# Modulation of the adaptive norm: from row products on GpSimd and ScalarE to matrix products on TensorE, weights through the weight ring

## The chip, the cores and the metric

The kernel runs on one core of one Trainium2 chip. The metric is the device time of one execution in microseconds (us), from the first to the last instruction of the core, as the median of several executions. Engines are called by the profile's names: PE is TensorE (matrix products), PEld its loads of the stationary operand, DVE is VectorE, ACT is ScalarE, POOL is GpSimd, and SP is SyncE, whose queue issues the transfers (DMAs).

## The reference, cut to what matters

A sequence of 256 tokens with 1024 features goes through two layers of a first block (feed-forward, hybrid mixer, feed-forward), and then through two layers of a second block, beside a context sequence of 256 tokens. Layer 0 of the second block is an RWKV mixer, layer 1 a differential attention. Each layer of the second block has an adaptive norm: six vectors of 1024 numbers (shift, scale and gate, for the latents and for the context) come from two small products that depend on the inputs `c` and `c_ctx` alone.

```
for l in range(2):                                   # first block
    x = x + 0.5 * swiglu_ffn(rmsnorm(x, norm_ffn1[l]), ...)
    x = x + hybrid_mixer(rmsnorm(x, norm_mix[l]), ...)
    x = x + 0.5 * swiglu_ffn(rmsnorm(x, norm_ffn2[l]), ...)
x = rmsnorm(x, final_norm)
for i in range(2):                                   # second block
    mod  = silu(c) @ ada_w[i] + ada_b[i]             # [1024] @ [1024, 3072]
    shift, scale, gate = split(mod, 3)
    modc = silu(c_ctx) @ ada_w[i] + ada_b[i]
    shift_c, scale_c, gate_c = split(modc, 3)
    h  = rms_norm(x, norm_g[i]) * (1 + scale) + shift
    hc = rms_norm(xc, norm_g[i]) * (1 + scale_c) + shift_c
    y, yc = rwkv7_mixer(h, hc, ...) if i == 0 else diff_mixer(h, hc, ...)
    x = x + gate * y
    if i == 0: xc = xc + gate_c * yc
```

The change is about `mod` and `modc`: two matrices `ada_w[i]` of 1024 x 3072, 12.6 MB each, multiplied by two vectors.

## The kernel before, in words

Features lie on the 128 partitions, tokens along the free dimension; 1024 features are 8 tiles (`KD = 8`). All large products are made in float32r with both operands split into a high and a low part, three products for one: `mm3` issues high x high, high x low and low x high into the same sums.

**Weights.** The class `Weights` streams weight chunks in the order in which they are used (`plan_first`, `plan_second`). A chunk is a tile of 128 x 1024 numbers, 512 KB, in the first block (tiles `wraw`) and of 128 x 512, 256 KB, in the second (`vraw`). It lands in one of `nraw` raw tiles; ACT makes its high part (`emit_hi`: `whi<-wraw`), DVE its low part (`emit_lo`: `wlo<-wraw,whi`; in the mixers some pieces go to POOL), each piece 128 x 512. The raw tile is free once the low part is made. `RING, RING2 = (4, 5), (4, 4)`: four raw tiles and five pairs of parts in the first block, four and four in the second. A chunk added with `split=False` is used as it lies and holds its raw tile until the next chunk is asked for (`get`). All transfers are issued by SP, in one queue, in order: what waits for a free tile holds up what stands behind it.

**Order.** Nothing is scheduled by a compiler: the instructions stand on each engine as the Python code emits them. The code keeps a rough account of time (`Clock`) and uses it to decide what to emit next. Work off the main path is written as generators ("chains", each `yield` ends a step); `tick`, `until` and `arrive` emit the steps that the account holds to be ready, and pieces of the weight splitting.

**First block.** `ffn` makes 44 products of 8 x 3 matrix products [128 x 256] each (up), a SwiGLU for each pair, then 8 products of 22 x 3 (down): 1584 matrix products. `mixer` makes 20 column tiles of `w_in` (conv, pool, gate), then ten rounds of a gelu tile with the gate matrices of the recurrence (`wax`) before every fourth, a pool product (`pw`), ten gate tiles, and the products upwards and out: 1560 matrix products.

**Second block.** `rwkv` goes through eight pairs of heads (`j`): projections of both sequences (512 columns), a low-rank product (`lora`), the gate's projection, and chains (`prepare`, `products`, `inverse`, `recur`, `readout`) with small products; the results of the first pairs are stored by SP (`zs`). Then come the output product and the attention.

**The modulation before.** `ada` (line 1094) is one chain. It brings `c_ctx` and `c` to all partitions (1 MB), and `ada_w` as rows: 96 pieces of 128 output columns x 512 inputs, 256 KB each, through two tiles of its own (`adaw`). For each piece

```
G.tensor_tensor(out=prod, in0=raw, in1=cb[:, :, 512 * h:512 * h + 512], op=ALU.mult)
yield
load()
for q in range(2):
    A.activation(prod[:, q], prod[:, q], AF.Copy, accum_out=sums[:, i, q, h:h + 1])
```

so POOL multiplies 128 x 1024 numbers, and ACT sums them in two passes (the tiles `cb` and `prod` are both called `ada` in the profile). The chain takes a step only while `self.calm` is set, which `ffn` sets and clears at its last down product: it runs beside the feed-forward stages, and stands still in the mixers. The last piece of a layer is followed by four or five small DVE instructions that make `mods` and `gs`. They are needed from `enter_ctx` on (layer 0), and after the RWKV stage (layer 1).

All operations go through one helper, so the profile gives line 89 for each of them; the tile names tell them apart.

## Time and profile before

| what | value |
|---|---|
| median of 3 timed executions | 2275.19 us (2267.83 to 2288.46) |
| span of the profiled execution, first to last instruction | 2274.9 us |
| its own time beside that | none is listed; the span stands 0.3 us under the median |
| mean granted clock of PE | 0.930 of 2.4 GHz |
| busy: PE, PEld | 2106.3 us (93%), 1882.8 us (83%) |
| busy: DVE, ACT, POOL | 1717.8 us (76%), 1287.4 us (57%), 861.8 us (38%) |
| moved by DMA | 300.41 MB, mean 132 GB/s |
| `ada` on POOL | 96 instructions, 238.7 us busy |
| `ada` on ACT | 192 passes, 118.7 us busy, and 192 reads of the sums, 35.8 us |

Busy times are unions of the instructions of an engine. PE's matrix products overlap, so that one of 0.28 us follows the one before by less than half of that: PE's idle time and the count of products in a stretch say more than its busy share. The granted clock of a stretch is a mean of two levels, 1 (2.4 GHz) and 0.5 (1.2 GHz). Idle time of an engine is put down to what ended it.

### The profile page before, as it was taken

How to read it: one execution, taken by the hardware profiler on the slowest of the kernel's cores; microseconds unless marked ns; L12 is line 12 of the kernel's file. 1: busy time of each engine (PE TensorE's matmuls, PEld its weight loads, DVE VectorE, ACT ScalarE, POOL GpSimd, SP SyncE). 2: the span in 40 equal slices, each digit the busy share in tenths (PEclk: the TensorE clock that was granted, in tenths of full speed). 3: DMA queues.
4: the chain of work that ended last, by engine and by line, in shares of the span. 5: the costliest groups of instructions: out<-in, count | busy, mean ns of one | idle time of the engine just before them, and what ended most of it. 6: DMA issues, size and time to landing. Idle time of an engine off the chain costs nothing. (4 is left out here: it accounts for less than half of the span.)

```text
span 2274.9 us, 47231 instructions
## 1 busy us (share of the span) xinstructions
PE 2106.3 (93%) x18172; PEld 1882.8 (83%) x18172; DVE 1717.8 (76%) x3076; ACT 1287.4 (57%) x2970; POOL 861.8 (38%) x1063
## 2 busy tenths in 40 slices
PE   8998998998889889989999988999999998999998
PEld 7988988998889889989999967677677667777878
DVE  6689898888878888897666675765766764558896
ACT  6666684666666666765556543354454342347565
POOL 1154565344544453562001153443543542312331
PEclk9999999999999999999999996899889877869999
DMA  7666554666666565456566310101100110215542
GB/s 243 207 190 202 159 167 131 213 204 200 195 211 209 189 199 193 149 156 197 187 187 183 121 57 24 34 25 39 38 28 30 32 40 9 59 52 165 148 121 89
DMA packets 114098, 300.41 MB, mean 132 GB/s; under 512 B 12624, under 2 KB 18512, under 8 KB 113744
## 3 DMA queue, kind: packets, MB, share of 16 engines
q1 hardware_dynamic: 113872, 297.39, 41.5%
q8 instruction: 142, 2.33, 0.4%
q14 instruction: 84, 0.69, 0.1%
HBM read 292.89 MB, written 4.46 MB: 131 GB/s over the span
## 5 line engine op out<-in xcount | busy, mean ns | idle before, releaser
L89 PE MATMUL ps<-ops,whi 128*128 128x256 f32 x4852 | 895.7, 282 | 19.9 <-ACT ops L89 9.2
L89 DVE TENSOR_TENSOR wlo<-wraw,whi 128x512 fp32r<-128x512 f32 (+2 forms) x792 | 675.4, 890 | 152.0 <-ACT whi L89 147.1
L89 PEld LDWEIGHTS ps<-ops,whi 128*128 128x128 f32 x4852 | 759.2, 190 | 23.9 <-ACT ops L89 9.4
L89 PE MATMUL ps<-ops,wlo 128*128 128x256 f32 x2504 | 710.2, 284 | 28.0 <-DVE wlo L89 28.0
L89 ACT ACTIVATE whi<-wraw 128x512 fp32r<-128x512 f32 (+2 forms) x798 | 437.4, 597 | 130.2 <-issue 60.2
L89 PEld LDWEIGHTS ps<-ops,wlo 128*128 128x128 f32 x2504 | 477.0, 191 | 35.4 <-DVE wlo L89 35.1
L89 PE MATMUL ps<-b,whi 128*128 128x256 f32 x1580 | 322.7, 290 | 31.8 <-ACT b L89 16.8
L89 POOL TENSOR_TENSOR ada<-adaw,ada 128x1024 f32<-128x1024 f32 x96 | 238.7, 2486 | 267.1 <-ACT ada L89 187.9
L89 PEld LDWEIGHTS ps<-b,whi 128*128 128x128 f32 x1580 | 262.2, 197 | 36.3 <-ACT b L89 17.4
L89 PE MATMUL ps<-ops,vhi 128*128 128x512 f32 (+1 forms) x624 | 228.9, 437 | 0.7 <-DVE ops L89 0.7
L89 PE MATMUL ps<-b,wlo 128*128 128x256 f32 x712 | 206.6, 290 | 9.7 <-DVE wlo L89 6.1
L89 DVE TENSOR_TENSOR vlo<-vraw,vhi 128x512 fp32r<-128x512 f32 x202 | 147.0, 740 | 26.3 <-ACT vhi L89 23.0
L89 POOL TENSOR_TENSOR small<-small,mhalf 128x8 f32<-128x8 f32 (+3 forms) x62 | 72.7, 1178 | 243.3 <-DVE small L89 243.1
L89 POOL TENSOR_TENSOR sq<-sq,t 128x256 f32<-128x256 f32 x49 | 45.2, 922 | 279.6 <-ACT t L89 279.1
L89 PEld LDWEIGHTS ps<-b,wlo 128*128 128x128 f32 x712 | 139.8, 196 | 13.5 <-DVE wlo L89 9.4
L89 ACT ACTIVATE ada<-ada 128x512 f32<-128x512 f32 (+1 forms) x193 | 120.6, 627 | 53.2 <-POOL ada L89 53.1
L89 PEld LDWEIGHTS ps<-ops,vhi 128*128 128x128 f32 x624 | 117.2, 201 | 27.2 <-DVE ops L89 1.5
L89 ACT ACTIVATE vhi<-vraw 128x512 fp32r<-128x512 f32 x202 | 121.4, 618 | 28.0 <-PE ps L89 13.7
L89 PE MATMUL ps<-ops,vlo 128*128 128x512 f32 (+1 forms) x312 | 133.5, 428 | 0.2 <-DVE vlo L89 0.2
L89 PE MATMUL ps<-vhi,ops 128*128 128x512 f32 x384 | 126.4, 408 | 2.8 <-ACT ops L89 1.4
L89 ACT ACTIVATE b<-t 128x256 fp32r<-128x256 f32 (+1 forms) x104 | 42.4, 412 | 100.7 <-DVE t L89 100.7
L89 PEld LDWEIGHTS ps<-vhi,ops 128*128 128x128 f32 x384 | 70.2, 190 | 22.1 <-ACT ops L89 3.9
(319 smaller groups left out, 3526.7 us busy)
## 6 DMA issues: line engine op xcount, KB each, us to landing
wraw<-in_ffn_w_up_dram SPq DMA_DIRECT2D x175, 512.0 KB, 3.7
wraw<-in_w_in_dram SPq DMA_DIRECT2D x80, 512.0 KB, 4.0
wraw<-in_ffn_w_down_dram SPq DMA_DIRECT2D x64, 512.0 KB, 3.6
adaw<-in_ada_w_dram SPq DMA_DIRECT2D x96, 256.0 KB, 3.9
vraw<-in_da_in_dram SPq DMA_DIRECT2D x96, 256.0 KB, 2.7
vraw<-in_rw_in_dram SPq DMA_DIRECT2D x60, 256.0 KB, 2.6
wraw<-in_ffn_w_down_dram SPq DMA_DIRECT2D x32, 384.0 KB, 3.6
wraw<-in_w_lru_up_dram SPq DMA_DIRECT2D x32, 320.0 KB, 2.9
```

Source lines behind the costliest of these rows:

```text
L89: return call(*args, **kw)
```

## The change

`ada_w` is now laid out like the other weights, with inputs on the partitions, and comes as unsplit chunks through the common rings. PE multiplies: the weight tile [128 inputs x 128 outputs] is the stationary operand, `silu` of the two vectors (128 x 2) the moving one, in plain float32, eight products for 128 outputs, so 24 x 8 = 192 for a layer and 384 in all. Layer 0's 24 column tiles stand in the mixers, 12 in each: one after each gelu tile, two after the pool product. Layer 1's stand in the RWKV stage, three for each pair of heads, between the low-rank product and the gate's projection, each as two chunks of 256 KB. DVE adds the bias out of PSUM (`ada_out`). The chain on POOL and ACT, its tiles and its 97 transfers are gone, and the first block's ring has six raw tiles for four. The `Clock` gets a price for such narrow products.

```diff
+        elif n <= 2:
+            self.clock.product(111, 4 * n, rows)
...
                         tiles(("gelu", l, i), "w_in", l, 14 + i)
+                        W.add(("ada", 0, 12 * l + i), a["ada_w"][0, 12 * l + i], split=False)
                     W.add(("pw", l), a["pool_w"][l])
+                    for i in (12 * l + 10, 12 * l + 11):
+                        W.add(("ada", 0, i), a["ada_w"][0, i], split=False)
...
             self.gemm([(w, 0)], xs, lambda _, ps: self.chain(gelu(t, ps)))
+            self.ada(W, 0, [12 * l + t])
...
             self.chain(pool_up(g, ps))
+        self.ada(W, 0, [12 * l + 10, 12 * l + 11])
...
-    def ada(self, pool):
...
+    def ada_setup(self):
...
+        self.cc = self.const.tile([128, KD, 2], F32, name="cc")
+        self.nc.sync.dma_start(out=self.cc, in_=self.a["cc"].rearrange("p (k q) -> p k q", q=2))
+        self.clock.end = self.clock.load(1 << 13)
+        yield
+        self.nc.scalar.activation(self.cc, self.cc, AF.Silu)
...
+    def ada(self, W, l, ids):
...
+        ps = self.take("ps")
+        for n, i in enumerate(ids):
+            for h in range(1 if l == 0 else 2):
+                w = W.get(("ada", l, i) if l == 0 else ("ada", l, i, h))
+                self.arrive(w.t)
+                nk = w[0].shape[1]
+                for k in range(nk):
+                    self.nc.tensor.matmul(ps[:, 2 * n:2 * n + 2], w[0][:, k, :], self.cc[:, nk * h + k, :],
+                                          start=h + k == 0, stop=nk * h + k == KD - 1)
+                    self.between()
+                self.tick()
+        self.chain(self.ada_out(l, ids, ps))
...
+    def ada_out(self, l, ids, ps):
...
+        V.tensor_tensor(out=m[:, i:i + n], in0=ps[:, 0:2 * n].rearrange("p (i q) -> p i q", q=2),
+                        in1=col("ada_b_2", 24 * l + i, n), op=ALU.add)
+        self.give(ps, kind="ps")
+        if ids[-1] == 23:
...
             W.add(("lora", j), a["rw_lora"][j])
+            for i in range(3 * j, 3 * j + 3):
+                for h in range(2):
+                    W.add(("ada", 1, i, h), a["ada_w"][1, i][:, 512 * h:512 * h + 512], split=False)
...
                 self.chain(out(d, j, *pss, ws))
                 self.tick()
+            self.ada(W, 1, [3 * j, 3 * j + 1, 3 * j + 2])
...
-        "ada_w": z["ada_w_2"].reshape(2, 2, 512, 24, 128).transpose(0, 3, 1, 4, 2),
+        "ada_w": tiles(z["ada_w_2"]),
...
-                K.chain(K.ada(wa), urgent=False, start=90000.0)
+                K.chain(K.ada_setup(), urgent=False, start=90000.0)
...
-RING, RING2 = (4, 5), (4, 4)
+RING, RING2 = (6, 5), (4, 4)
```

Three places show how the order moves. The first is POOL's order before, from the down products of the second feed-forward stage of layer 0 into the next stage; `sq<-sq` adds squares for the norm, `small` is its root.

```order
L89 TENSOR_TENSOR ada_1346<-adaw_1348,ada_1345 128x1024
L89 TENSOR_TENSOR sq<-sq,t_136 128x256
L89 TENSOR_TENSOR ada_1346<-adaw_1347,ada_1345 128x1024
L89 TENSOR_TENSOR ada_1346<-adaw_1348,ada_1345 128x1024
L89 TENSOR_TENSOR sq<-sq,t_137 128x256
L89 TENSOR_TENSOR sq<-sq,t_129 128x256
L89 TENSOR_TENSOR ada_1346<-adaw_1347,ada_1345 128x1024
L89 TENSOR_TENSOR ada_1346<-adaw_1348,ada_1345 128x1024
L89 TENSOR_TENSOR sq<-sq,t_127 128x256
L89 TENSOR_TENSOR ada_1346<-adaw_1347,ada_1345 128x1024
L89 TENSOR_TENSOR small_73<-small_73,mhalf 128x2
L89 TENSOR_TENSOR ada_1346<-adaw_1348,ada_1345 128x1024
```

This is POOL's order now at the same place.

```order
L89 TENSOR_TENSOR sq<-sq,t_130 128x256
L89 TENSOR_TENSOR sq<-sq,t_126 128x256
L89 TENSOR_TENSOR sq<-sq,t_129 128x256
L89 TENSOR_TENSOR sq<-sq,t_127 128x256
L89 TENSOR_TENSOR sq<-sq,t_128 128x256
L89 TENSOR_TENSOR sq<-sq,t_124 128x256
L89 TENSOR_TENSOR small_73<-small_73,mhalf 128x2
```

The products of `adaw` are gone from between the sums and from ahead of the root. The second place is PE's order before in the RWKV stage, second pair of heads: the end of the low-rank product (`lora`) and the gate's projection (`ops`, 512 columns).

```order
L89 MATMUL ps_90<-lora_15867,vhi 128x512
L89 MATMUL ps_90<-lora_15867,vlo 128x512
L89 MATMUL ps_96<-lora_15869,vhi 128x512
L89 MATMUL ps_96<-lora_15869,vlo 128x512
L89 MATMUL ps_91<-ops_84,vhi 128x512
L89 MATMUL ps_91<-ops_85,vhi 128x512
L89 MATMUL ps_91<-ops_84,vlo 128x512
```

This is PE's order now there, from the narrow products on (`cc` is the moving operand, `vraw` the unsplit weights); `ident` marks transposes of the chains.

```order
L89 MATMUL ps_90<-ident,q_15706 128x128 x4
L89 MATMUL ps_93<-cc,vraw 128x2 x16
L89 MATMUL ps_94<-ident,q_15706 128x128 x4
L89 MATMUL ps_89<-ident,vp_15703 128x128 x4
L89 MATMUL ps_92<-ident,q_15708 128x128 x4
L89 MATMUL ps_93<-cc,vraw 128x2 x8
L89 MATMUL ps_96<-ident,q_15708 128x128 x4
L89 MATMUL ps_94<-hind,w_15697 128x2 x4
L89 MATMUL ps_89<-ident,vp_15703 128x128 x4
L89 MATMUL ps_90<-ops_84,vhi 128x512
```

Four chunks' products stand together, two chunks' follow behind twelve transposes, and the gate's projection comes after them. The third place is SP's queue before in the RWKV stage, around the first two stores of results (`zs`).

```order
L173 DMA vraw<-in_rw_in_dram 128x512 x5
L1783 DMA zs_107<-s_15821 128x512
L173 DMA vraw<-in_rw_in_dram 128x512 x3
L173 DMA vraw<-in_rw_lora_dram 128x512
L173 DMA vraw<-in_rw_in_dram 128x512 x4
L1783 DMA zs_108<-s_15824 128x512
```

This is SP's queue now, around the same two stores.

```order
L175 DMA vraw<-in_ada_w_dram 128x512 x3
L1790 DMA zs_107<-s_15686 128x512
L175 DMA vraw<-in_ada_w_dram 128x512 x3
L175 DMA vraw<-in_rw_in_dram 128x512 x8
L175 DMA vraw<-in_rw_lora_dram 128x512
L175 DMA vraw<-in_ada_w_dram 128x512 x4
L1790 DMA zs_108<-s_15689 128x512
L175 DMA vraw<-in_ada_w_dram 128x512 x2
```

The stores now stand between the chunks of one group of narrow products, with the last of these and the gate's weights behind them.

## Rows read from the trace of the kernel before

**Rows 1.** Busy time by stage: stretch, length, engines with counts, clock, DMA share, GB/s.

```profile
core 0: us, PE busy (x) PEld busy (x) DVE busy (x) ACT busy (x) POOL busy (x), PEclk, DMA share, GB/s
18.00:108.00 90.00, 89.08 (x762) 88.77 (x761) 63.80 (x135) 52.76 (x108) 10.98 (x19) 1.00 0.65 211
108.00:225.00 117.00, 105.02 (x839) 102.73 (x837) 100.18 (x148) 75.55 (x181) 54.89 (x89) 0.96 0.63 199
225.00:433.00 208.00, 193.70 (x1551) 189.30 (x1551) 183.38 (x312) 134.41 (x294) 110.97 (x138) 0.97 0.53 166
433.00:658.00 225.00, 199.13 (x1614) 194.59 (x1613) 191.07 (x234) 144.98 (x359) 106.08 (x49) 0.96 0.62 200
658.00:873.00 215.00, 194.03 (x1566) 190.46 (x1567) 181.76 (x232) 140.12 (x346) 95.75 (x45) 0.96 0.64 206
873.00:1081.00 208.00, 192.97 (x1574) 188.36 (x1574) 179.50 (x311) 134.20 (x293) 107.16 (x137) 0.98 0.52 166
1081.00:1268.00 187.00, 186.62 (x1585) 186.41 (x1586) 123.84 (x239) 105.61 (x213) 13.59 (x15) 1.00 0.58 178
1287.00:2046.00 759.00, 702.70 (x7246) 537.89 (x7245) 486.77 (x1027) 332.36 (x805) 298.26 (x513) 0.84 0.13 41
```

**Rows 2.** The same for the tile ada alone: ACT busy, POOL busy.

```profile
433.00:658.00 225.00, 53.15 (x160) 99.03 (x40) 0.96 0.62 200
658.00:873.00 215.00, 49.12 (x148) 88.94 (x36) 0.96 0.64 206
```

**Rows 3.** DVE groups, stretches 433:658, 658:873, 1081:1268: busy, mean ns | idle before.

```profile
L89 DVE TENSOR_TENSOR wlo<-wraw,whi 128x512 fp32r<-128x512 f32 x129 | 140.3, 1119 | 27.8 <-ACT whi L89 27.3
...
L89 DVE TENSOR_TENSOR wlo<-wraw,whi 128x512 fp32r<-128x512 f32 x129 | 132.3, 1056 | 22.7 <-ACT whi L89 22.0
...
L89 DVE TENSOR_TENSOR wlo<-wraw,whi 128x512 fp32r<-128x512 f32 x128 | 83.6, 691 | 47.5 <-ACT whi L89 47.4
```

**Rows 4.** Timeline of 575:590, POOL and DVE: start, length, instruction, count.

```profile
575.54 2.41 POOL L89 TENSOR_TENSOR ada<-adaw,ada 128x1024 f32<-128x1024 f32 x1 [2.69 <-ACT ada L89]
...
575.97 2.87 DVE L89 TENSOR_TENSOR wlo<-wraw,whi 128x512 fp32r<-128x512 f32 x2 [0.36 <-ACT whi L89]
...
584.73 1.28 DVE L89 TENSOR_TENSOR wlo<-wraw,whi 128x512 fp32r<-128x512 f32 x2
```

**Rows 5.** PE's waits in 433:658, 658:873 (two rows), 1081:1268: us, times, longest.

```profile
PE ps L89 <- DVE wlo L89: 11.6, 13, 2.0
...
PE ps L89 <- POOL sq L89: 6.7, 1, 6.7
PE ps L89 <- ACT b L89: 6.2, 1, 6.2
...
PE ps L89 <- DVE ops L89: 0.4, 1, 0.4
```

**Rows 6.** Timeline of PE around 1270: four narrow float32 products, and the next.

```profile
1270.51 0.59 PE L89 MATMUL ps<-mean,sqf 128*128 128x2 f32 x4
1270.96 0.36 PE L89 MATMUL ps<-ops,whi 128*128 128x256 f32 x1
```

**Rows 7.** Busy time in the gelu and gate part of layer 0's mixer.

```profile
303.00:368.00 65.00, 59.65 (x482) 58.24 (x481) 64.81 (x109) 48.48 (x104) 41.46 (x47) 0.97 0.52 158
```

**Rows 8.** RWKV stage, 1287:2046: SP's waits, and transfers with us to landing.

```profile
SPq L173 <- DVE vlo L89: 594.3, 75, 55.9
SPq L1783 <- DVE s L89: 36.2, 4, 12.4
...
vraw<-in_rw_in_dram SPq DMA_DIRECT2D x56, 256.0 KB, 2.6
```

**Rows 9.** Groups of the page: the split of the second block's weights.

```profile
L89 DVE TENSOR_TENSOR vlo<-vraw,vhi 128x512 fp32r<-128x512 f32 x202 | 147.0, 740 | 26.3 <-ACT vhi L89 23.0
...
L89 ACT ACTIVATE vhi<-vraw 128x512 fp32r<-128x512 f32 x202 | 121.4, 618 | 28.0 <-PE ps L89 13.7
```

**Rows 10.** Timeline of DVE: a small instruction that reads PSUM.

```profile
660.77 0.16 DVE L89 TENSOR_SCALAR small<-ps 128x4 f32<-128x4 f32 x1 [0.82 <-PE ps L89]
```

More of the change, by code (lines that the diff above doesn't have):

```diff
@@ L1041 @@
 ATTENTION = (2, 0, 4, 6, 3, 1, 5, 7)
-NRAW = 2
 EARLY = 32, 33, 8, 0
@@ L1092, in setup_second @@
         yield
-    def ada(self, pool):
-        nc, V, A, G = self.nc, self.nc.vector, self.nc.scalar, self.nc.gpsimd
-        cb, prod = [pool.tile([128, 2, n], F32, name=f"ada{n}") for n in (1024, 512)]
-        raws = [pool.tile([128, 512], F32, name=f"adaw{i}") for i in range(NRAW)]
-        sums = self.const.tile([128, 24, 2, 2], F32, name="adas")
-        nc.sync.dma_start(out=cb, in_=self.a["cc"].rearrange("o (q k) -> o q k", q=2).to_broadcast([128, 2, 1024]))
-        self.clock.end = self.clock.load(1 << 20)
-        yield
-        A.activation(cb, cb, AF.Silu)
-        work = [(l, i, h) for l in range(2) for i in range(24) for h in range(2)]
-        there = []
-        def load():
-            n = len(there)
-            if n < len(work):
-                nc.sync.dma_start(out=raws[n % NRAW], in_=self.a["ada_w"][work[n]])
-                there.append(self.clock.load(1 << 18))
-        for _ in range(NRAW):
-            load()
-        for n, (l, i, h) in enumerate(work):
+    def ada_setup(self):
+        self.cc = self.const.tile([128, KD, 2], F32, name="cc")
+        self.nc.sync.dma_start(out=self.cc, in_=self.a["cc"].rearrange("p (k q) -> p k q", q=2))
+        self.clock.end = self.clock.load(1 << 13)
+        yield
+        self.nc.scalar.activation(self.cc, self.cc, AF.Silu)
@@ L1116, in ada @@
+    def ada_out(self, l, ids, ps):
+        V, n, i = self.nc.vector, len(ids), ids[0]
+        col = lambda name, k, n: self.P(name, k, n).rearrange("p (i o) -> p i o", o=1).to_broadcast([128, n, 2])
+        m = self.mods[:, l]
+        V.tensor_tensor(out=m[:, i:i + n], in0=ps[:, 0:2 * n].rearrange("p (i q) -> p i q", q=2),
+                        in1=col("ada_b_2", 24 * l + i, n), op=ALU.add)
+        self.give(ps, kind="ps")
+        if ids[-1] == 23:
             yield
-            while not self.calm or there[n] > self.clock.t["PE"]:
-                yield
@@ L1119, in ada @@
-            raw = raws[n % NRAW].rearrange("p (o k) -> p o k", o=1).to_broadcast([128, 2, 512])
-            G.tensor_tensor(out=prod, in0=raw, in1=cb[:, :, 512 * h:512 * h + 512], op=ALU.mult)
+            V.scalar_tensor_tensor(out=self.gs[:, l], in0=m[:, 8:16], scalar=1.0, in1=col("norm_g_2", KD * l, KD),
+                                   op0=ALU.add, op1=ALU.mult)
             yield
-            load()
-            for q in range(2):
-                A.activation(prod[:, q], prod[:, q], AF.Copy, accum_out=sums[:, i, q, h:h + 1])
@@ L1125, in ada @@
-            if i == 23 and h == 1:
-                yield
-                m = self.mods[:, l]
-                V.tensor_tensor(out=m, in0=sums[:, :, :, 0], in1=sums[:, :, :, 1], op=ALU.add)
-                col = lambda name, k, n: self.P(name, k, n).rearrange("p (i o) -> p i o", o=1).to_broadcast([128, n, 2])
-                V.tensor_tensor(out=m, in0=m, in1=col("ada_b_2", 24 * l, 24), op=ALU.add)
-                V.scalar_tensor_tensor(out=self.gs[:, l], in0=m[:, 8:16], scalar=1.0, in1=col("norm_g_2", KD * l, KD),
-                                       op0=ALU.add, op1=ALU.mult)
-                if l == 0:
-                    V.tensor_tensor(out=self.gsx, in0=self.gs[:, 0, :, 1], in1=self.P("final_norm", 0, KD), op=ALU.mult)
+            if l == 0:
+                V.tensor_tensor(out=self.gsx, in0=self.gs[:, 0, :, 1], in1=self.P("final_norm", 0, KD), op=ALU.mult)
@@ L2247, in layout @@
         "rw_lora": np.concatenate([lora, lora], axis=1),
-        "ada_w": z["ada_w_2"].reshape(2, 2, 512, 24, 128).transpose(0, 3, 1, 4, 2),
-        "cc": np.concatenate([z["c_ctx_2"].reshape(1, -1), z["c_2"].reshape(1, -1)], axis=1), "da_in": blocks(z["da_in_2"][0]),
+        "ada_w": tiles(z["ada_w_2"]),
+        "cc": np.stack([z[n].reshape(KD, 128) for n in ("c_ctx_2", "c_2")], axis=2).transpose(1, 0, 2).reshape(128, -1),
+        "da_in": blocks(z["da_in_2"][0]),
         "da_out": blocks(z["da_out_2"][0]).transpose(1, 0, 2, 3),
@@ L2277, in build @@
                 pool = lambda name: c1.enter_context(tc.tile_pool(name=name, bufs=1))
-                wa, K.big, K.tmp, wp = pool("wa"), pool("big"), pool("tmp"), pool("wp")
+                K.big, K.tmp, wp = pool("big"), pool("tmp"), pool("wp")
                 K.temps(K.tmp, 12)
```

## The prediction

> **What bounds the kernel now.** I read the busy times by stage first. The three feed-forward stages 18:225, 433:658 and 658:873 and the one at 1081:1268 make the same 1584 products, but take 207, 225, 215 and 187 us [rows 1]. The last is nearly PE alone: busy for 186.62 of 187 us at clock 1.00, one product per 187/1585 = 0.118 us. The others lose time to idle PE and to a lower granted clock (down to 0.96). The first stage holds its own control: up to 108 us PE is busy for 89.08 of 90 us at clock 1.00, after it for 105.02 of 117 us at 0.96. What differs is the chain `ada`: it starts at 108 us, runs beside 433:658 and 658:873 (POOL 99.03 and 88.94 us, ACT 53.15 and 49.12 us [rows 2]), and is over before 1081.
>
> Next, how it reaches PE, in the groups of DVE by line. The same piece of weight splitting, `wlo<-wraw,whi` of 128x512, takes 1119 and 1056 ns in the mean beside `ada` and 691 ns without [rows 3]; so DVE, which makes every low part, has 129 x 0.43 = 55 us more to do in 433:658. The timeline shows single cases: two such pieces begun 0.4 us after a POOL product of 2.41 us take 2.87 us, and two with POOL idle 1.28 us [rows 4]. DVE stands while POOL's product runs. Last, the waits of PE: in 433:658 it waits 11.6 us in 13 pieces for `wlo`, and once 6.2 us for a part of the SwiGLU, behind the same late DVE; a row just like this one stands in 658:873. At the head of 658:873 it waits 6.7 us for the squares' sum on POOL, which stands behind `ada` products there. In 1081:1268 the largest is 0.4 us [rows 5]. So beside `ada` the bound is the pair of DVE and POOL, elsewhere in the feed-forward stages PE itself.
>
> The mixers (208 us each) are another case: no `ada` runs there, and yet between 303 and 368 us DVE is busy for 64.81 of 65 us and PE issues only 482 products [rows 7], where the pace above would give 65/0.118 = 551. The RWKV stage is long (759 us), with PE busy for 702.70 us at a mean clock of 0.84 and DMA at 0.13 [rows 1].
>
> **The change part by part.**
>
> *The chain on POOL and ACT goes.* Its own busy time is not the gain; the gain is what the stages lose beside it. First stage, from 108 us on: idle 117 - 105.0 = 12.0 us, and clock 0.04 x 117 = 4.7 us, together 17. Second: 225 - 187 = 38 us (25.9 idle, 9.0 clock, and 29 records of products more at 0.118, which is 38 again). Third: 215 - 187 = 28. Sum 83 us. I take all of it, because the stage without `ada` has nothing late next: PE is at 99.8% there, with the four raw tiles of the old ring. For the lower bound I leave the waits that name another engine than DVE: 6.2 twice and 6.7 make 19, so 64.
>
> *Layer 0's products come into the mixers.* No row has this operation, but a near one is four float32 products with a moving operand of 128x2 and a full stationary tile: from 1270.51 to the next at 1270.96, 0.1125 us each [rows 6]. A mixer gets 12 x 8 x 0.1125 = 10.8 us of PE. The room there is (551 - 482) x 0.118 = 8.1 us in the stretch that holds the ten gelu tiles' end, the pool product and the gate tiles; DVE is the bound and has no splitting to do for the new chunks. That leaves 2.7 us. DVE gets 12 additions out of PSUM, 0.16 us each [rows 10], 1.9 us on the engine that is full. 4.6 us for each mixer, 9 for both. Bounds: 0, and 10.8 + 1.9 = 12.7 each, 25. The 6.3 MB more in a mixer bring its 166 GB/s to some (166 x 208 + 6300)/208 = 196, below the 206 of a feed-forward stage [rows 1], so I cost them at nothing; if they gathered in the gelu rounds, PE would wait there and the room would be smaller, up to the same bound.
>
> *Layer 1's products come into the RWKV stage.* 192 x 0.1125 = 21.6 us. PE is busy for 702.7 of 759 us, 93%, so 20 us if they fall anywhere. Lower bound 0: the stage also has idle time behind its chains, and the new products wait for nothing but weights. Upper bound from the ring of four raw tiles, if no chain's products fill the waits: a chunk's four products take 0.45 us; the fifth chunk can be asked for only when the first is used, and lands 2.6 us later [rows 8], at 3.05, while PE is through with four at 1.8; the sixth ends at 3.95. The gate's first chunk is asked for when the third is used, at 1.35, lands at 3.95 and is split in 0.62 + 0.74 us [rows 9], ready at 5.3. So 5.3 us for each pair of heads, 42 in all. I take 20, nearer to the products' price, since the order puts transposes and other chain products between the chunks.
>
> *What else moves.* SP is rid of 97 transfers in the feed-forward stages. In RWKV its five stores now stand between chunks of a group: behind a waiting store lie the last chunks and the gate's weights, for which PE waits. Before, SP waited 36.2 us in four cases for such stores [rows 8], but with 594.3 us of waits for raw tiles beside them it had time. I cost this at nothing in the sum and make a rival of it. The two raw tiles more, the transposed layout and `silu` on 16 columns cost nothing: the cover is that no stage shows PE waiting for a transfer. The sum over all: 2274.9 - 83 + 9 + 20 = 2221 us, against a span that lies 0.3 us under the median of the runs.
>
> **The rivals.**
>
> *All of the new work is hidden.* 2274.9 - 83 = 2192. For it: PE's gaps in both places. Against: PE stands at 93% in RWKV.
>
> *RWKV pays for feeding or for the clock.* 2274.9 - 83 + 9 + 42 = 2243. For it: four raw tiles and six chunks in a row. A lower clock gives the same size: the stage's mean is 0.84, and 0.80 would cost 0.04 x 759 = 30 us beside the 20, so 2251. The Trainium skill, page "TensorE: Matmul & The Clock Gate", section "HAM oscillation — how this bites in real kernels", says that thin products with waits for transfers between them fall back to the low clock again and again; the trace of before has no such group, so it can't confirm it. Against both: the groups are some 3 us of the 92 us for each pair.
>
> *The stalls stay in part, since not `ada` makes them.* POOL also adds squares, and the change of stages has waits of its own: gain 64, so 2274.9 - 64 + 9 + 20 = 2240. Against: the last stage has these too, and no stalls.
>
> *Slower: the stores block the ring.* Where SP reaches a store before its result is there, the fifth and sixth chunk and the gate's weights come late, and PE, which issues in order, stands at the narrow products with all chain work behind it. Price: 36.2/4 = 9.05 us for each of five stores, 45, beside the 42 of feeding: 2274.9 - 83 + 9 + 87 = 2288. It decides from 83 - 9 = 74 us in the stage, 9.3 for each pair. Against: a store is emitted only when the account holds its result for made.
>
> *Each narrow float32 product goes through the array four times.* 384 x 0.45 = 173 us with no room for it: 2274.9 - 83 + 4 + 173 = 2369. Rows 6 speak against it: same type, same shape of both operands, 0.1125 us each. The Trainium skill, page "FP8 and Floating Point Precision", section "TensorE Precision Notes", has true FP32 as four passes; by that rule the change loses, by the row it wins, and the row decides.
>
> **How the numbers follow.** Chances: the forecast (2221, within 2203 to 2239) 0.66; feeding or clock 0.15; stalls stay in part 0.07; all hidden 0.06; stores 0.05; four passes 0.01. The likeliest is 2221. From 2190 (all hidden) to 2254 (the clock's case with 3 us to spare) the range leaves out the stores, the four passes and the tails, and takes in the bounds of the mixers. A change of 1%, 23 us, is about what a measurement here tells from none, so faster ends at 2252. Faster: the forecast, all hidden and most of the next two, 0.86. Same: the rest of these and the stores, 0.11. Slower: 0.03.
>
> **What would show it.** In the changed profile the first three feed-forward stages should take 187 to 192 us each (from 18 us on), with `wlo` near 0.69 us and clock 1.00; the `cc` products should start some 0.11 us apart; each mixer should take 208 to 221 us, and RWKV 759 to 801. It is wrong if `wlo` stays above 0.9 us in the feed-forward stages, or if PE's waits for `vraw` in RWKV add up to more than 74 us.

## The result, and the profile after

The change makes the kernel slower: 2338.75 us in the median (2332.47 to 2342.54, 4 runs) against 2271.51 of the kernel before on the same chip, a ratio of 1.0276 with a 95% interval of 1.0229 to 1.0324. Predicted were 2221 us, 2190 to 2254. In what follows one per cent of the kernel before is 22.7 us; ratios leave disturbed runs out, so they can differ a little from the ratio of two medians, and most in the run called "order of no layer 1" below, where two of four runs count. The profiled execution of the changed kernel has a span of 2340.6 us.

Busy time by stage of the changed kernel, with the columns of [rows 1] (the first stage is not cut in two here, and the last row is the attention):

```profile
core 0: us, PE busy (x) PEld busy (x) DVE busy (x) ACT busy (x) POOL busy (x), PEclk, DMA share, GB/s
18.00:208.00 190.00, 189.16 (x1566) 189.16 (x1567) 131.17 (x281) 103.85 (x209) 17.92 (x88) 0.99 0.62 191
208.00:428.00 220.00, 214.76 (x1772) 213.08 (x1771) 176.35 (x325) 134.83 (x293) 102.51 (x137) 0.98 0.57 185
428.00:617.00 189.00, 189.00 (x1578) 189.00 (x1578) 122.29 (x227) 98.71 (x196) 6.20 (x8) 1.00 0.62 184
617.00:808.00 191.00, 191.00 (x1596) 191.00 (x1595) 122.75 (x229) 98.50 (x198) 6.05 (x8) 1.00 0.60 183
808.00:1027.00 219.00, 213.88 (x1775) 211.30 (x1774) 180.87 (x326) 135.48 (x294) 103.40 (x138) 1.00 0.58 185
1027.00:1217.00 190.00, 190.00 (x1588) 190.00 (x1587) 123.31 (x239) 105.65 (x212) 12.95 (x14) 1.00 0.56 170
1237.00:2112.00 875.00, 821.27 (x7654) 647.75 (x7652) 501.88 (x1059) 340.74 (x821) 307.40 (x512) 0.77 0.16 51
2112.00:2340.00 228.00, 210.62 (x1217) 175.19 (x1217) 179.74 (x375) 138.55 (x315) 58.37 (x48) 0.96 0.42 127
```

Read the lengths first. The four feed-forward stages take 190, 189, 191 and 190 us, where they took 207, 225, 215 and 187 [rows 1]. PE is busy from end to end there. The mixers take 220 and 219 us for 208, and the RWKV stage takes 875 us for 759. So the gain came where it was forecast, and more than all of it went again in one stage. In that stage the clock is 0.77 for 0.84, PE is as busy as before (821.27 of 875 us is 94%, for 93%), and the DMA share is 0.16: PE does not wait more, it runs slower. A smaller loss stands in the feed-forward stages. PE is busy nearly without a gap in them at a clock of 0.99 and 1.00, and yet a product takes 191/1596 = 0.120 us where the control stage of the prediction had 0.118; what sets this pace no run shows.

The group of DVE that carried the gain, in the second of the feed-forward stages (mean ns behind the busy time):

```profile
L89 DVE TENSOR_TENSOR wlo<-wraw,whi 128x512 fp32r<-128x512 f32 x128 | 83.0, 688 | 49.5 <-ACT whi L89 49.4
```

688 ns where it was 1119 [rows 3]: the low parts are made at their own pace again.

The new products in the first mixer, on PE's timeline (start, length, instruction, count):

```profile
271.23 0.28 PE L89 MATMUL ps<-ops,wlo 128*128 128x256 f32 x1
271.35 1.84 PE L89 MATMUL ps<-cc,wraw 128*128 128x2 f32 x16
273.05 0.36 PE L89 MATMUL ps<-ops,whi 128*128 128x256 f32 x1
```

This is one column tile. The code makes eight `matmul` calls for it, one for each row tile, and the row has sixteen records, from 271.35 to 273.05: 1.70 us, 0.106 us for each record and 0.21 us for each **call**. One float32 product of the code is two records of PE. [Rows 6] said so already: four records with `sqf` come from only two calls in `two_norms` (two parts of 128 tokens), and the prediction took them for four calls.

The same tile in the RWKV stage (records of both engines, least, median and longest ns, and what its engine waited for):

```profile
L89 PEld LDWEIGHTS ps<-cc,vraw x384: 186/286/338, 1254.0 to 1886.3; 128*128 128x128 f32 x192
L89 PE MATMUL ps<-cc,vraw x384: 167/352/374, 1254.3 to 1886.4; 128*128 128x2 f32 x192
its engine sat idle before it (us, times) until:
  DMA vraw<-in_ada_w_dram: 3.0, 2
```

192 calls, 384 records, and 3.0 us of waits for their weights in two cases. The least and the longest weight load, 186 and 338 ns, are of one and the same form. SP's waits for the stores of the stage:

```profile
SPq L1790 <- DVE s L89: 29.1, 4, 15.3
```

29.1 us in four cases, for 36.2 before [rows 8]. Neither waits for the new weights nor the stores are what the stage loses.

### The profile page after: what moved, and what is told of

Same layout as the page of the kernel before. It is cut to its first block, busy times and chain, and to the rows that moved or that the text cites. A ratio compares the mean times of both kernels' runs of the same rounds, so it can differ in the third digit from the quotient of the medians.

```text
span 2340.6 us, 48235 instructions
## 1 busy us (share of the span) xinstructions
PE 2247.3 (96%) x18940; PEld 2033.1 (87%) x18940; DVE 1560.6 (67%) x3104; ACT 1179.0 (50%) x2584; POOL 623.1 (27%) x967
## 4 chain that ended last, share of the span: by engine, by line
PE 80%; DVE 10%; POOL 5%; issue 3%; ACT 2%; DMA 1%; SPq 0%; DVEq 0%; ACTq 0%; POOLq 0%
PE ps L89 80%; POOL invX L89 2%; POOL invt L89 2%; DVE q L89 1%; DVE t L89 1%; DVE invN L89 1%; DVE vlo L89 1%; DVE wlo L89 1%; DVE X L89 1%; DVE GE L89 1%; DVE small L89 1%; DVE b L89 1%; DVE aq L89 1%; DVE s L89 1%; DVE w L89 1%
## 5 line engine op out<-in xcount | busy, mean ns | idle before, releaser
L89 PE MATMUL ps<-ops,whi 128*128 128x256 f32 x4852 | 907.8, 283 | 10.7 <-ACT ops L89 7.0
L89 DVE TENSOR_TENSOR wlo<-wraw,whi 128x512 fp32r<-128x512 f32 (+2 forms) x793 | 535.5, 713 | 232.5 <-ACT whi L89 226.3
L89 PEld LDWEIGHTS ps<-ops,wlo 128*128 128x128 f32 x2504 | 471.4, 188 | 7.4 <-DVE wlo L89 7.1
L89 PE MATMUL ps<-b,whi 128*128 128x256 f32 x1580 | 311.3, 284 | 3.3 <-DVE b L89 3.3
L89 PEld LDWEIGHTS ps<-b,whi 128*128 128x128 f32 x1580 | 255.1, 192 | 4.5 <-DVE b L89 4.3
L89 PE MATMUL ps<-ops,vhi 128*128 128x512 f32 (+1 forms) x624 | 238.5, 455 | 0.0
L89 PEld LDWEIGHTS ps<-ops,vhi 128*128 128x128 f32 x624 | 126.0, 214 | 30.6 <-issue 2.2
L89 DVE TENSOR_TENSOR S<-Sd,ps 64x64 f32<-64x64 f32 x224 | 48.8, 218 | 79.0 <-PE ps L89 73.4
L89 DVE TENSOR_SCALAR uv<-ps 64x64 f32<-64x64 f32 x137 | 30.1, 219 | 98.9 <-PE ps L89 89.9
L89 ACT ACTIVATE rs<-ps 64x128 f32<-64x128 f32 x104 | 28.1, 270 | 133.3 <-PE ps L89 121.0
```

Of the source, the lines that this page charges most:

```text
L89: return call(*args, **kw)
```

## The experiments

Each edit is against the changed kernel, except where it says the kernel before. To compare the RWKV stage I take it here from the final norms' products to the first product `ps<-vhi,ops`, with which the attention's own products begin; with the columns of [rows 1] that is, for the kernel before and then for the changed one:

```profile
1270.00:2044.00 774.00, 718.10 (x7388) 553.64 (x7386) 496.45 (x1055) 340.41 (x823) 298.55 (x513) 0.84 0.13 40
```

```profile
1220.00:2101.00 881.00, 828.48 (x7764) 658.24 (x7764) 506.02 (x1075) 341.82 (x824) 308.42 (x513) 0.77 0.16 50
```

774 us at 0.84 and 881 us at 0.77. PE is idle for 55.9 us of the first and 52.5 us of the second: the added 107 us are not waits. The table gathers all runs; "length x clock" is the stage's length at the full clock, if PE alone set it. Stage and clock come from one profiled execution of each run, which can lie up to 21 us off the median beside it.

| run | median us | ratio to before | stage us | clock | length x clock |
|---|---|---|---|---|---|
| the kernel before | 2272 | 1 | 774 | 0.84 | 650 |
| the changed kernel | 2339 | 1.028 | 881 | 0.77 | 678 |
| before, no chain | 2194 | 0.964 | 762 | 0.86 | 655 |
| before, no chain, order of no layer 1 | 2238 | 0.979 | 792 | 0.82 | 649 |
| before, no chain, another order | 2209 | 0.971 | 767 | 0.86 | 660 |
| before, new price | 2272 | 1.001 | 788 | 0.81 | 638 |
| change, no layer 1 | 2265 | 0.994 | 821 | 0.79 | 649 |
| change, layer 1 without loads | 2349 | 1.033 | 882 | 0.77 | 679 |
| change, layer 1 wide | 2288 | 1.007 | 828 | 0.85 | 704 |
| change, old price | 2303 | 1.014 | 842 | 0.80 | 674 |
| change, another order | 2297 | 1.011 | 826 | 0.83 | 686 |
| change, one product a call | 2258 | 0.996 | 805 | 0.84 | 676 |
| wide, old price, charged as narrow | 2272 | 1.002 | 798 | 0.88 | 702 |
| wide, old price, charged as wide | 2235 | 0.986 | 763 | 0.92 | 702 |
| wide, old price, charged as wide, another order | 2228 | 0.981 | 761 | 0.92 | 700 |
| one product a call, wide, old price | 2221 | 0.979 | 784 | 0.86 | 674 |

The last column has three levels, whatever the order: 638 to 660 without layer 1's products, 674 to 686 with narrow ones or with one product a call, 700 to 704 with wide ones at two products a call. So the stage's work hardly varies, and the granted clock decides its length.

**The chain alone.** The kernel before without `ada`:

```diff
+        V.memset(self.mods, 0.1)
+        V.memset(self.gs, 1.0)
+        V.memset(self.gsx, 1.0)
...
-                K.chain(K.ada(wa), urgent=False, start=90000.0)
```

> The kernel before without its modulation chain on GpSimd and ScalarE, for both layers; the modulation columns are constants. The prediction's first term says that the chain costs 83 us, all of it in the three feed-forward stages that lie beside it: 2271.5 - 83 = 2189 us, with each of them near 190 us and the RWKV stage unchanged at 759 us. If the gain in the feed-forward stages is given back by a later stage that starts earlier, the RWKV stage grows and the run ends above 2210 us.

2193.83 us, ratio 0.9638 (0.9597 to 0.9679): 3.6%, 82 us. In its profile the final norms, which end the first block, come at 1188 us, for 1270 [rows 6]. The term of 83 us holds.

**Without layer 1.**

```diff
+        V.memset(self.mods[:, 1], 0.1)
+        V.memset(self.gs[:, 1], 1.0)
...
-            for i in range(3 * j, 3 * j + 3):
-                for h in range(2):
-                    W.add(("ada", 1, i, h), a["ada_w"][1, i][:, 512 * h:512 * h + 512], split=False)
...
-            self.ada(W, 1, [3 * j, 3 * j + 1, 3 * j + 2])
```

> The changed kernel without layer 1's modulation: its 24 column tiles are neither loaded nor multiplied, and its modulation columns are constants. Every theory that puts the loss on layer 1's products in the RWKV stage (their own time at two hardware products each, the clock they lower, the feeding of their tiles) expects that stage back near the 759 us of the kernel before, with the granted clock near 0.84, and a time of 2338.75 - 116 = 2223 us. If the loss sits elsewhere, for instance in where the first block now ends against the RWKV stage's own chains, the stage stays above 820 us.

2265.01 us, ratio 0.9944 (0.9903 to 0.9984). The expectation failed: 74 us come back, not 116, and the stage stays far above 759.

```profile
1219.00:2040.00 821.00, 759.82 (x7381) 585.54 (x7380) 504.37 (x1060) 341.94 (x824) 300.76 (x512) 0.79 0.12 38
```

The stage has no product here that it does not have in the kernel before, and takes 821 us at 0.79 (the profiled run is the longest of its ten, 18 us over their median). So a part of the loss can come without the new products. But leaving them out also changes the order of the others: the two traces have 7358 of the stage's other products in common, and no more than 5710 of them stand in the same sequence. So this run against the changed kernel shows layer 1's products and a change of order in one.

**Layer 1 without its loads.** One resident piece of weights for all tiles:

```diff
+class Pairs:
...
+        return self.t[:, at[1] % 2, :]
...
-                w = W.get(("ada", l, i) if l == 0 else ("ada", l, i, h))
+                w = W.get(("ada", l, i)) if l == 0 else [Pairs(self.adw)]
```

> The changed kernel with layer 1's 384 product calls kept, but all from one resident piece of weights (so layer 1's modulation is not the reference's): no transfers, no ring slots and no stretch of the ring taken by unsplit tiles. Feeding theory (the ring of four is full of modulation tiles, so the split of the next projection tiles starts late): the RWKV stage falls from 875 to 790 us or less, the run to 2255 us or less. Price and clock theories: the stage stays within 15 us of 875, the run at 2325 to 2345 us.

2348.59 us, ratio 1.0329 (1.0293 to 1.0364).

```profile
1220.00:2102.00 882.00, 828.12 (x7772) 657.12 (x7770) 504.13 (x1075) 338.32 (x818) 301.00 (x508) 0.77 0.11 36
```

882 us at 0.77, with a DMA share of 0.11 for 0.16, and a run that is no faster. The order of the other products is another one here too, so this alone would not do; with the 3.0 us of waits for the weights, and with PE's idle time no longer than before, it shows that feeding is not the cause.

**Layer 1 in wide products.**

```diff
+                        cw = self.cc[:, nk * h + k, :].rearrange("p (o q) -> p o q", o=1).to_broadcast([128, 64, 2])
+                        self.clock.product(111, 8, 128)
+                        self.nc.tensor.engine.matmul(ps[:, 128 * n:128 * n + 128], w[0][:, k, :], cw,
+                                                     start=h + k == 0, stop=nk * h + k == KD - 1)
...
```

> The changed kernel with layer 1's products made 128 columns wide (the two columns repeated 64 times by a stride of zero); the planner is charged the same, the number of hardware products is the same, and a 128-column float32 product costs about 109 ns at full clock by a row of the trace, as much as a narrow one. Clock theory (the narrow products are what lowers the RWKV stage's granted clock from 0.84 to 0.77): the clock comes back to 0.82 to 0.86 and the stage from 875 to 790 to 820 us, the run to 2255 to 2285 us. Price theory (what is lost is the time of 768 hardware products and of what stands behind them): same, 2330 to 2345 us. If the wide products take twice as long at half clock, slower by up to 40 us.

2288.25 us, ratio 1.0067 (1.0029 to 1.0104): 2.1%, some 50 us less than the changed kernel, with the same order of products row by row. That is 3 us over the range of the clock theory, and 42 us under that of the price theory.

```profile
1218.00:2046.00 828.00, 770.59 (x7766) 603.48 (x7766) 505.40 (x1075) 342.41 (x824) 305.86 (x513) 0.85 0.17 53
```

The clock comes back from 0.77 to 0.85. The products themselves, busy time of the tile `cc` on PE and PEld, in the changed kernel and then here:

```profile
1220.00:2101.00 881.00, 70.99 (x384) 67.50 (x384) 0.00 (x0) 0.77 0.16 50
```

```profile
1218.00:2046.00 828.00, 58.09 (x384) 48.43 (x384) 0.00 (x0) 0.85 0.17 53
```

The 384 records with 64 times the columns take less time, 58.09 us for 70.99. The median load of their weights takes 191 ns, where it took 286 in the changed kernel:

```profile
L1120 PEld LDWEIGHTS ps<-cc,vraw x384: 186/191/337, 1252.3 to 1838.6; 128*128 128x128 f32 x192
```

One place shows how it comes about. These are two stretches of the third pair of heads, one after the other, in the changed kernel and then here; layer 1's products stand among small products of the chains, in the same sequence in both.

```profile
1366.00:1374.00 8.00, 8.00 (x83) 6.75 (x81) 3.56 (x14) 2.81 (x8) 2.18 (x3) 1.00 0.19 59
1374.00:1386.00 12.00, 12.00 (x72) 10.68 (x71) 2.66 (x13) 3.57 (x9) 0.74 (x2) 0.51 0.25 73
```

```profile
1362.40:1370.40 8.00, 8.00 (x81) 6.71 (x80) 3.48 (x14) 2.80 (x8) 2.26 (x3) 1.00 0.17 51
1370.40:1378.00 7.60, 7.60 (x75) 6.46 (x74) 2.83 (x13) 3.58 (x10) 0.74 (x2) 1.00 0.40 121
```

In both PE is busy for all of the first 8 us, at a clock of 1.00. Then the clock falls to 0.51 with narrow products and stays at 1.00 with wide ones, and the same work takes 12.00 us for 7.60, in which PE is never idle. So narrow products lower the clock against wide ones, for themselves and for all that runs beside them. Against none at all it is not shown in one order: without layer 1, in the other order, the clock was 0.79, so that wide products also raise it. The Trainium skill, page "TensorE: Matmul & The Clock Gate", section "HAM oscillation — how this bites in real kernels", puts such a fall down to a TensorE that waits for transfers between bursts of thin products. Here it came without such waits: PE was busy throughout in the rows above, it waited 3.0 us for these weights in the whole stage, and the clock was 0.77 with none of their loads either.

**The new price in the kernel before.**

```diff
+        elif n <= 2:
+            self.clock.product(111, 4 * n, rows)
```

> The kernel before with one thing of the change: the planner's new price for float32 products of at most two columns (111 ns for 214). The kernel before has such products as well, four for each pair of heads in the chain that prepares a pair and a few in the norms, so its order changes from the first pair on; no instruction is added or taken away. Order theory (the RWKV stage of the changed kernel is slower even without layer 1's products because the new price lays its chains another way): slower than before by 20 to 50 us, 2293 to 2323, with the loss in the RWKV stage at a lower granted clock. If the price is harmless, 2265 to 2280 us.

2272.04 us, ratio 1.0010 (0.9973 to 1.0048). No loss: the order theory's expectation failed, and another order as such costs nothing there. The profiled run, with 788 us at 0.81, is the longest of its ten, 21 us over their median.

**The order of the run without layer 1, in the kernel before.** The kernel before without the chain, with the new price and, from the RWKV stage on, the planner's state of the changed kernel:

```diff
...
+                K.clock.t.update({'PE': 1099710.698, 'V': 1094364.458, 'A': 1090651.386, 'G': 1077339.292, 'DMA': 1060233.304})
+                K.clock.now, K.clock.columns, K.clock.fast = 322, 1305.0, True
...
```

> The kernel before without its modulation chain (constants for the modulation columns), with the new price and with the planner's state at the start of the RWKV stage set to what it is in the changed kernel; TensorE's products from there on then stand in the very order of the changed kernel without layer 1's products, row by row. The two differ in the first block alone. Order theory: the RWKV stage and the attention take what they take there, 20 to 45 us more than without the new price, so 2214 to 2239 us against 2194. If the order is worth nothing and the loss comes over from the first block by another way, 2185 to 2200 us.

2238.2 us, ratio 0.9792 (0.9706 to 0.9877), against 0.9638 (0.9597 to 0.9679) with the order of before: 1.5%, 35 us. In the traces the stage's products stand in the sequence of the run without layer 1; the changed kernel's own order, with layer 1's products left out of account, is a third one. The stage of the run without the chain, and of this one:

```profile
1188.00:1950.00 762.00, 705.57 (x7384) 544.33 (x7383) 496.24 (x1055) 340.18 (x823) 298.26 (x513) 0.86 0.13 41
```

```profile
1188.00:1980.00 792.00, 732.57 (x7388) 565.03 (x7386) 501.24 (x1060) 342.22 (x824) 302.87 (x512) 0.82 0.13 40
```

The same instructions, 762 us at 0.86 and 792 us at 0.82. So an order can be worth this much. What the changed kernel's own order costs, this run does not show.

**Two more orders.** Half of one of the planner's ticks as an offset from the RWKV stage on, in the kernel before without the chain and in the changed kernel:

```diff
-        now = int(max(self.t["PE"], self.base) / self.TICK)
+        now = int((max(self.t["PE"], self.base) - self.phase) / self.TICK)
...
+                K.clock.phase = 1700.0
```

> The kernel before without its modulation chain, old price; only the planner's account of the array's clock is shifted by half of one of its ticks from the start of the RWKV stage on. No instruction is added or taken away, the order from the first pair of heads on is another. Lottery theory (any other order of the RWKV stage can be worth some 40 us either way, since the granted clock depends on it): anywhere from 2185 to 2245 us, and away from 2194 by over 15. If only the order of the new price is bad: 2185 to 2205 us.

2209.2 us, ratio 0.9714 (0.9636 to 0.9791). The interval overlaps that of the run without the offset: inconclusive.

> The changed kernel, as it is, with the same shift of the planner's account from the RWKV stage on: the same instructions in another order. Lottery theory: the 44 us that the order of the changed kernel costs come back in part, 2295 to 2330 us. If layer 1's products lose their 74 us and the order its 44 in any order, 2330 to 2350 us.

2296.82 us, ratio 1.0110 (1.0011 to 1.0208): 1.7%, some 40 us less than the changed kernel with its own order.

```profile
1220.00:2046.00 826.00, 783.85 (x7771) 623.22 (x7769) 488.48 (x1029) 353.33 (x864) 292.15 (x506) 0.83 0.17 54
```

826 us at 0.83, in the fastest of the four runs, 17 us under their median. The changed kernel had an order that is worse than this other one.

**The old price.** The two lines of the price taken out of the change:

```diff
-        elif n <= 2:
-            self.clock.product(111, 4 * n, rows)
```

> The changed kernel without the planner's new price: a product of two columns is charged 214 ns again, near the 225 ns that one call takes in the trace (two hardware products of 0.11 us). All instructions stay. Order theory: the RWKV stage gets 20 to 45 us back, the run 2294 to 2319 us. If what is lost beside layer 1's own products has nothing to do with the price, 2330 to 2345 us.

2302.76 us, ratio 1.0137 (1.0068 to 1.0206): 36 us less by the medians.

```profile
1227.00:2069.00 842.00, 806.05 (x7772) 639.33 (x7770) 492.48 (x1055) 354.61 (x859) 285.54 (x501) 0.80 0.17 53
```

842 us at 0.80. It is in the expected range, but the offset alone gave as much, so this is no proof that the price was the fault.

**One hardware product for each call.**

```diff
-                        W.add(("ada", 0, 12 * l + i), a["ada_w"][0, 12 * l + i], split=False)
+                        W.add(("ada", 0, 12 * l + i), a["ada_w"][0, 12 * l + i], split="hi")
...
+        cc, self.cc = self.cc, self.const.tile([128, KD, 2], F32R, name="ccr")
```

> The changed kernel with the modulation products in one hardware product for each call: ScalarE rounds the weight tile to float32r, silu gives float32r columns, and the low part of the weights is left out. 384 narrow products remain of 768. Price theory: each layer gives back half of its 43 us of TensorE, so 2339 - 43 = 2296 us. Clock theory: layer 1's half also gives back half of the 50 us that wide products gave, so 2339 - 43 - 25 = 2271 us. If ScalarE's 0.6 us for each piece of 512 columns costs as much as it saves, 2325 us or more.

2258.37 us, ratio 0.9957 (0.9924 to 0.9990): 80 us less than the changed kernel, and more than either theory expected (43 and 68). The final norms on PE's timeline, which end the first block: without layer 1 but with layer 0, here, and without both layers.

```profile
1218.83 0.36 PE L89 MATMUL ps<-mean,sqf 128*128 128x2 f32 x2
```

```profile
1198.44 0.36 PE L89 MATMUL ps<-mean,sqf 128*128 128x2 f32 x2
```

```profile
1188.09 0.36 PE L89 MATMUL ps<-mean,sqf 128*128 128x2 f32 x2
```

1218.8, 1198.4 and 1188.1 us. Half of layer 0's records are 192, and 192 x 0.1125 = 21.6 us; the first block is 20.4 us shorter. The agreement is luck, as the stages show. Here are the first mixer and the feed-forward stage behind it, cut at the norms' products, without layer 1 and then in this run:

```profile
210.30:429.50 219.20, 214.69 (x1768) 213.17 (x1767) 175.68 (x324) 134.49 (x292) 103.29 (x137) 0.98 0.56 185
429.50:619.60 190.10, 190.10 (x1588) 190.10 (x1587) 122.85 (x228) 99.78 (x198) 6.07 (x8) 1.00 0.61 185
```

```profile
206.30:424.50 218.20, 204.94 (x1673) 201.31 (x1672) 180.40 (x324) 146.38 (x316) 103.81 (x137) 0.98 0.58 186
424.50:611.00 186.50, 186.50 (x1588) 186.50 (x1587) 122.69 (x228) 99.48 (x198) 6.05 (x8) 1.00 0.62 188
```

The mixer, which has half as many of the new records, is 1.0 us shorter (the second one 4.6), and PE is idle in it for 13.3 us where it was for 4.5. The feed-forward stage, which has none of them, is 3.6 us shorter, with the same 1588 products at the same clock; the four together are some 14 us shorter. So this run mixes three things, fewer records, a faster pace elsewhere for a reason that no run shows, and another order in the RWKV stage, and it does not price a record.

**Both remedies, and what the planner is charged.** Wide products and the old price; first charged by the planner as the wide products that they are:

```diff
+                    if l == 1:
+                        c, n0 = c.rearrange("p (o q) -> p o q", o=1).to_broadcast([128, 64, 2]), 128 * n
+                    self.nc.tensor.matmul(ps[:, n0:n0 + (128 if l == 1 else 2)], w[0][:, k, :], c,
```

> The changed kernel with layer 1's products 128 columns wide and charged as such, and without the new price for the others: both remedies in one. If the 36 us of the price and the 50 us of the wide products are separate causes, they add: 2339 - 36 - 50 = 2253 us. If both give back the same lost clock, about what the better of them gives, 2280 to 2300 us.

2235.13 us, ratio 0.9860 (0.9762 to 0.9959), 18 us below the 2253 at which the two gains would just add, with the stage at a clock of 0.92:

```profile
1222.00:1985.00 763.00, 723.19 (x7764) 568.50 (x7763) 490.88 (x1044) 349.61 (x850) 294.06 (x508) 0.92 0.18 57
```

Then with `self.clock.product(214, 8, 128)`, as narrow ones, and with the true charge and an offset of half a tick:

> The changed kernel without the new price, layer 1's products 128 columns wide, but charged by the planner as products of two columns at the old price: the order of the run with the old price alone, to the row, with wide products in it. If the wide products alone made the gain of the run with both remedies, 2230 to 2255 us. If the planner has to know of the wide products (their columns in its account of the clock), or that run's order was a lucky one, 2260 to 2300 us.

> The run with both remedies, with the planner's account of the clock shifted by half of one of its ticks from the RWKV stage on: the same instructions in another order. If its 2235 us and the granted clock of 0.92 come from an account that tells the truth about layer 1's products, 2220 to 2250 us again. If they were the luck of one order, 2260 to 2290 us, near the 2288 us of the wide products in the changed kernel's own order.

Charged as narrow ones: 2271.83 us, ratio 1.0015 (0.9982 to 1.0048).

```profile
1224.00:2022.00 798.00, 753.00 (x7768) 590.35 (x7767) 493.69 (x1053) 353.24 (x856) 288.18 (x501) 0.88 0.18 56
```

Charged as wide ones, another order: 2227.69 us, ratio 0.9808 (0.9747 to 0.9868).

```profile
1225.00:1986.00 761.00, 719.92 (x7765) 566.32 (x7764) 486.40 (x1049) 350.12 (x847) 300.84 (x504) 0.92 0.19 58
```

761 us at 0.92 again, and 798 us at 0.88 with the wrong charge. Both orders with the true charge give 0.92; the two with the charge of narrow products, this one and that of the first wide run, give 0.88 and 0.85. The runs with the true charge are 1.5% and 2.1%, 35 and 47 us, faster than the one with the wrong charge. That speaks for the charge; but with two orders of each kind, where one order against another has been worth 35 to 40 us, it is no proof. With layer 1's products in it, the stage is about as long as before the change (774).

**One product a call, wide, old price.** The edit of the run with one hardware product and that with wide ones together.

> One hardware product for each call (weights rounded to float32r by ScalarE, their low part left out), layer 1's 128 columns wide, and the old price. The products' own time is 21 us for each layer at full clock. From the time of before without the chain, 2194 + 21 + 14 in the first block = 2229 us if the granted clock of the RWKV stage is that of before; each 0.01 of that clock is worth some 9 us, so 2229 to 2260 us. It should be the fastest of all kernels that compute both layers.

2221.16 us, ratio 0.9792 (0.9708 to 0.9877), 8 us below the expected range and the lowest median of all that compute both layers, but with the weights' low part left out. The two runs at full precision, 2235 and 2228, are within its interval.

## Why the prediction was wrong, step by step

*The chain goes, 83 us.* Right, in size and place: 82 us with the chain simply left out, and the feed-forward stages at 189 to 191 us in the changed kernel.

*Layer 0 in the mixers, 9 us.* Wrong by a factor, in one step: "0.1125 us each" is the price of a record, and a call has two. With 0.225 us the working as it stood gives 21.6 - 8.1 + 1.9 = 15.4 us for each mixer, 31 for both. The profiles show 1218.8 - 1188.1 = 30.7 us, the ratios 0.9944 - 0.9792, 35 us. That the sum comes so close is in part luck: without the chain the mixers take 205.8 and 208.3 us, and with layer 0's products 219.2 and 219.4, so they have 24.5 of the 30.7 us, and the rest stands in the feed-forward stages, which have none of these products. The room and the DVE term are not shown by themselves. The loss is also above the upper bound of 25, which hung on the same reading.

*Layer 1 in the RWKV stage, 20 us.* The same step makes it 43.2 x 93% = 40. Measured, with layer 1 against without it: 1.0276 - 0.9944, 3.3%, 75 us, in which a change of order is included. Wide products, as many and in the changed kernel's own order, take 1.0276 - 1.0067, 47 us, of them away. These 47 us are the clock that narrow products lose against wide ones: the step that failed here is the last part of "I take 20, nearer to the products' price", which let new products cost their own time alone, in a stage whose length is work divided by a clock that they change. The other 28 us are the time of the products and whatever the further change of order costs or gives; no run parts these two.

*What else moves, nothing.* This left out a term. The change puts the RWKV stage's other products in another order, and an order alone was worth 35 us (0.9792 - 0.9638) with no new product in it. That was the order of the run without layer 1; the changed kernel's own order is some 40 us worse than the one with the offset. The prediction did not weigh the planner's price and its account at all.

The terms, from ratios: -82 (the chain) + 35 (the order of the run without layer 1) + 35 (layer 0) + 28 (layer 1 in wide products, with the order that goes with them) + 47 (narrow for wide) = +63 us, and 2.76% of 2272 is 63. Each term is the step from one run to the next, so that they must add up; what they show is where the time goes. With the one misread row put right, the sum of the prediction would have been 2274.9 - 83 + 31 + 40 = 2263, no change. What makes it slower is the clock, by the products' width as shown, and by the order, as far as the runs part it.

*The rivals.* Feeding is refuted by 3.0 us of waits for the weights and by the run without loads, the stores by 29.1 us of waits for 36.2. The rival of the clock was the right mechanism with too small a price: 0.04 for 0.07 (0.84 to 0.77). The four passes came near in time, 2369, but with 0.45 us a call for the 0.21 measured, and without the clock. The Trainium skill, page "FP8 and Floating Point Precision", section "TensorE Precision Notes", has four passes for true FP32; the records here are two for each call, and how many passes stand behind a record no run shows.

*What would show it.* Stages at 187 to 192 us, `wlo` at 0.69, `cc` records 0.11 us apart, mixers of 208 to 221 us: all came, and they could not show the wrong price, since the spacing was read for a call. The lengths of the RWKV stage told it, 875 for 801 at most. Waits for `vraw` did not.

What stays open: which places in an order lower the clock, what the changed kernel's own order costs apart from its new products, and why the feed-forward stages run at another pace from program to program. That an order alone can lower the clock is shown; that a true charge for the products keeps it up was so in both orders tried.

## What to carry to other kernels

Before a row prices a new instruction, count the calls in the code against the records in the row. A stage that is bound by TensorE below its full clock is worth length times clock: price what a product takes, and then ask what it does to the clock of everything beside it; a product with few columns can be cheaper when it is made wide. Where a planner orders the work, its charge for a new instruction is part of the change: give it the measured price, and try the change in a second order before it is judged. And before a saving is put down to fewer instructions, see that it stands in the stage that has them.

## What the runs showed of the hardware

A float32 product of 128x128 weights with 2 columns is two records of 0.106 us at the full clock of 2.4 GHz, 0.21 us a call. With 128 columns (384 records) PE was busy for 58.09 us where 2 columns took 70.99, as the mean clock was 0.85 for 0.77. The weight load took 186 ns at the least in either case, 338 and 337 at the most, and 286 and 191 in the median. In one place of the stage PE was busy without a gap for 8 us at a clock of 1.00; then the clock fell to 0.51 with products of 2 columns and stayed at 1.00 with 128, still without a gap.

Two programs with the same instructions and another order of one stage differed by 35 us, and by some 40 in another pair, with granted clocks of 0.86 and 0.82, and 0.83 and 0.77, in that stage.

The same 1588 products of a feed-forward stage took 190.10 us in one program and 186.50 in another, with PE busy throughout and a clock of 1.00 in both; the cause is not known.
